# A hybrid attention, RWKV and gated-delta block on one core: wider tail products, and a fixed TensorE order of dense runs and small pieces

## Chip, cores, metric

The kernel runs on one core of a Trainium2 chip. The metric is the device time of one execution in microseconds (us); the median of three runs counts.

## What is computed

One transformer block over 1024 tokens of width 1024 in float32. The normalised input is projected once; three branches then mix the tokens, each of width 512, and a gated sum, an output projection and a feed-forward part follow:

```python
h = _rms(x, norm_mix_g[i])
proj = h @ w_in[i]
...
o_a = _nsa(...)      # 8 heads: compressed, selected and windowed attention
o_b, v_first = _rwkv7(...)   # 8 heads: a recurrence over the tokens
o_c = _gdn(...)      # 4 heads: a recurrence over chunks of the tokens
gate = jax.nn.sigmoid(p_gate.reshape(B, S, 3, D))
merged = (gate[:, :, 0] * (o_a @ w_branch[i, 0]) + gate[:, :, 1] * (o_b @ w_branch[i, 1])
          + gate[:, :, 2] * (o_c @ w_branch[i, 2]))
x = x + merged @ w_out[i]
h = _rms(x, norm_ffn_g[i])
x = x + jnp.square(jax.nn.relu(h @ w_ff1[i])) @ w_ff2[i]
```

## The kernel before

Large products are made from two halves of each operand: `whi` and `wlo` of a weight tile, `hTh` and `hTl` of the normalised input (`h2h`, `h2l` after the second norm, `fh`, `fl` of the hidden layer, `mh` and `ms` of the merged branches). Three matmuls of 128 x 128 weights per block make one product, and all add up in one PSUM tile `fps`. These are the **dense** matmuls. `load_w` fetches a weight tile (`wraw`), ScalarE casts it to `whi` (line 253), and GpSimd or VectorE or both subtract to get `wlo` (line 258); `TBUF` sets how many such pairs the tail keeps, `TRAW` how many raw tiles.

The **small pieces** are the matmuls and transposes of the three branches (`mps` tiles). They run in stages: RWKV up to 650 us (a step of its recurrence is `VS,AG`, then `xs,U`, then `VS,G`, with VectorE copies between), GDN from 690 to 1087 us (a step is `gZ,KQ`, `gxh,gU`, `gyb,gKg`; ahead of each unit a ladder of `gT`, `gU`, `gXb` inverts a triangular matrix), a preparation of the attention keys, then NSA with 32 units of two heads each (scores `K2s`, `K2w`, `K2c`; a VectorE maximum `ast`; a ScalarE exponential `P`; transposes of `P`; products `PH`, `PL` with the values).

A planner in the program, `Block.run`, emits the two kinds in turn. `Tensor` counts an estimated TensorE time; a task that yields a number is due again after that much estimated time. Small pieces add to `owed`, and where more than 0.64 us are owed, or no task is due, `dense_step` emits one step, which is three dense matmuls. Dense steps come from the branches' own projections and from a stock of 34 projections of gates and attention inputs (`waiting`), of which some are kept back (`keep`) until NSA begins. Emission is not yet the order: a scheduler behind it may move instructions by priority, and dense steps have a lower one. `Tensor.note` ties the first matmul of a dense step behind the last small piece emitted before it; nothing ties a small piece behind a dense one.

When the first half of NSA's units is emitted, `end_mixed` queues `tail(0)`: branch products, gates, output projection, second norm and feed-forward for the first 512 tokens, as dense work beside the second half of NSA. `tail(1)` does the same for the other 512 tokens at the end, where nothing else is left. Inside, `accum` adds products into the SBUF tile `acc`, 256 output columns at a time: for each of four row blocks all k steps run into one PSUM tile, then VectorE adds it to `acc`. The feed-forward part makes four hidden tiles (`up`, 24 matmuls each) and then their down products, eight groups per tail.

Of the kernel before, what the change touches and what calls it, by code (L numbers as in the profile page):

```python
# [42 lines left out]
FDIV = (0, 1)  # L43
TRAW = (2, 2)
TBUF = (2, 2)
# [3 lines left out]
OBUF = 5  # L49
# [32 lines left out]
class Tensor:  # L82
    EDGE = mybir.DependencyInfo(mybir.DependencyClass.NoSync, mybir.DependencyReason.DATA)

    def __init__(self, tc):
        self.tc, self.nc, self.time = tc, tc.nc, 0.0
        self.last = self.anchor = None
        self.dense = False

    def matmul(self, out, lhsT, rhs, **kw):  # L90
        m, n = lhsT.free_size(), out.free_size()
        if lhsT.dtype == F32:
            self.time += (2 * n + 64 if m <= 64 else 4 * max(n, P)) / 2400
        else:
            self.time += max(n, 64) / 2400
# [6 lines left out]
    def note(self, ins):  # L102
        if not self.dense:
            self.fresh = ins.ins
        elif self.anchor is not None:
            self.tc.add_manual_dep(ins.ins, self.anchor.name, self.EDGE, reason="dense step behind a small one")
            self.anchor = None
# [3 lines left out]
class Block:  # L111
# [54 lines left out]
    def run(self, until):  # L166
        now = lambda: self.te.time
        while not until():
            if self.owed > 0.64 and self.dense_step():
                self.owed -= 0.64  # L170
                continue
            can = [t for t in self.tasks if t.when is None or t.when()]
            due = [t for t in can if t.ready <= now()]
            if due:
# [5 lines left out]
                self.owed = min(self.owed + self.share * (now() - at), 2.0)  # L180
                if t.done:
                    self.tasks.remove(t)
            elif self.dense_step():
                self.owed = max(self.owed - 0.64, 0.0)
# [1226 lines left out]
    def tail(self, hf, wbufs):  # L1411
# [9 lines left out]
        def load(src, cols):  # L1421
            return self.load_w(src, 4, cols, wp, wbufs, TRAW[hf], div())

        with pool("tacc") as ap, pool("tw") as wp:
# [5 lines left out]
            def accum(lhs, w_rows, kt, c0):  # L1430
                ws = [load(w_rows[j * 512:(j + 1) * 512, c0:c0 + 256], 256) for j in range(kt // 4)]
                for st in range(4):
                    m = slice(st * P, (st + 1) * P)
                    ps = psum()[:, 0:256]
                    for k in range(kt):
                        (wh, wl), j = ws[k // 4], k % 4
                        self.te.matmul(ps, lhsT=lhs[0](k)[:, m], rhs=wh[:, j, :], start=(k == 0), stop=False)
                        self.te.matmul(ps, lhsT=lhs[0](k)[:, m], rhs=wl[:, j, :], start=False, stop=False)
                        self.te.matmul(ps, lhsT=lhs[1](k)[:, m], rhs=wh[:, j, :], start=False, stop=(k == kt - 1))
                        if k % 2:  # L1440
                            yield
                    tt(out=acc[:, st, c0:c0 + 256], in0=ps, in1=acc[:, st, c0:c0 + 256], op=OP.add)  # L1442
# [171 lines left out]
```

## Time and profile before

| | us |
|---|---|
| median of 3 runs | 2568.1 |
| lowest, highest | 2564.01, 2571.09 |
| profiled execution | 2570.32 |
| its span, first to last instruction | 2568.6 |
| TensorE matmuls busy | 2414.0 |
| VectorE busy | 1488.7 |
| ScalarE busy | 1044.3 |
| GpSimd busy | 989.9 |

Matmuls overlap in the records, so the time that one costs is the distance from its start to the next start, and not its duration. Idle time of TensorE is a stretch less its busy time. PE stands for TensorE, DVE for VectorE, ACT for ScalarE, POOL for GpSimd. A small float32 matmul appears as two records in the trace and as one row in the built order.

### The profile page before, as it was taken

How to read it: one execution, taken by the hardware profiler on the slowest of the kernel's cores; microseconds unless marked ns; L12 is line 12 of the kernel's file. 1: busy time of each engine (PE TensorE's matmuls, PEld its weight loads, DVE VectorE, ACT ScalarE, POOL GpSimd, SP SyncE). 2: the span in 40 equal slices, each digit the busy share in tenths (PEclk: the TensorE clock that was granted, in tenths of full speed). 3: DMA queues.
4: the chain of work that ended last, by engine and by line, in shares of the span. 5: the costliest groups of instructions: out<-in, count | busy, mean ns of one | idle time of the engine just before them, and what ended most of it. 6: DMA issues, size and time to landing. Idle time of an engine off the chain costs nothing.

```text
span 2568.6 us, 41137 instructions
## 1 busy us (share of the span) xinstructions
PE 2414.0 (94%) x15509; PEld 2013.4 (78%) x15509; DVE 1488.7 (58%) x3325; ACT 1044.3 (41%) x2085; POOL 989.9 (39%) x975
## 2 busy tenths in 40 slices
PE   7989899999898999989999999899999999999999
PEld 4767676777777777777887778788888878899988
DVE  4587877673576666223557787764454444545444
ACT  5333423332343333225667675753322333423232
POOL 4444433333322121234446675343332345223332
PEclk9889889999999999999999999899999999999999
DMA  4222222222223122362214331025322354223233
GB/s 135 66 54 66 57 52 66 70 55 79 67 66 83 40 54 76 114 137 76 61 50 141 101 102 37 20 72 154 95 91 86 104 160 132 78 87 107 83 104 102
DMA packets 340214, 217.05 MB, mean 84 GB/s; under 512 B 78486, under 2 KB 314144, under 8 KB 340016
## 3 DMA queue, kind: packets, MB, share of 16 engines
q1 hardware_dynamic: 329152, 195.63, 27.2%
q10 hardware_dynamic: 9792, 17.83, 1.9%
q8 instruction: 122, 2.00, 0.3%
q0 software_dynamic: 1072, 0.96, 0.2%
q14 instruction: 76, 0.62, 0.1%
HBM read 178.16 MB, written 36.22 MB: 83 GB/s over the span
## 4 chain that ended last, share of the span: by engine, by line
PE 71%; DVE 15%; DMA 6%; ACT 4%; issue 2%; POOL 1%; SPq 0%; ACTq 0%; DVEq 0%; POOLq 0%
PE fps L96 53%; PE mps L96 15%; PE mps L100 3%; DVE inv_p L335 2%; DVE inv_u L337 1%; DMA gin<-gates 1%; DVE BK L549 1%; DVE gacc L881 1%; DMA cw<-in_nsa_cmp_w_dram 1%; DMA lb<-inv 1%; ACT P L1348 1%; DMA inv<-LT 1%; DVE ast L1343 1%; DVE PL L1391 1%; DVE AG L536 1%
## 5 line engine op out<-in xcount | busy, mean ns | idle before, releaser
L258 POOL TENSOR_TENSOR wlo<-wraw,whi 128x512 fp32r<-128x512 f32 (+2 forms) x408 | 528.6, 1297 | 940.1 <-ACT whi L253 907.4
L253 ACT CAST whi<-wraw 128x512 fp32r<-128x512 f32 (+1 forms) x408 | 286.2, 703 | 699.5 <-PE fps L96 612.0
L96 PE MATMUL fps<-hTh,whi 128*128 128x512 f32 x1024 | 448.7, 440 | 6.7 <-ACT rraw L423 3.5
L96 PE MATMUL fps<-hTh,wlo 128*128 128x512 f32 x1024 | 416.4, 411 | 3.4 <-POOL wlo L258 3.4
L96 PE MATMUL fps<-hTl,whi 128*128 128x512 f32 x1024 | 418.1, 410 | 0.0
L96 PE MATMUL fps<-wlo,fh 128*128 128x256 f32 x1024 | 266.6, 284 | 7.0 <-DVE wlo L258 7.0
L96 PE MATMUL fps<-whi,fl 128*128 128x256 f32 x1024 | 266.7, 283 | 0.0
L96 PE MATMUL fps<-whi,fh 128*128 128x256 f32 x1024 | 266.0, 284 | 0.6
L258 DVE TENSOR_TENSOR wlo<-wraw,whi 128x256 fp32r<-128x256 f32 (+1 forms) x207 | 142.2, 690 | 180.2 <-ACT whi L253 180.1
L96 PEld LDWEIGHTS fps<-hTh,wlo 128*128 128x128 f32 x1024 | 200.7, 196 | 50.8 <-POOL wlo L258 5.2
L96 PEld LDWEIGHTS fps<-hTh,whi 128*128 128x128 f32 x1024 | 201.4, 197 | 49.0 <-ACT whi L253 3.8
L96 PEld LDWEIGHTS fps<-hTl,whi 128*128 128x128 f32 x1024 | 202.4, 198 | 32.5
L1442 DVE TENSOR_TENSOR acc<-fps,acc 128x256 f32<-128x256 f32 x288 | 118.6, 422 | 178.5 <-PE fps L96 178.1
L96 PE MATMUL fps<-h2h,whi 128*128 128x512 f32 x512 | 200.1, 391 | 0.9 <-DVE h2l L290 0.9
L96 PE MATMUL fps<-h2h,wlo 128*128 128x512 f32 x512 | 200.0, 391 | 0.2 <-DVE wlo L258 0.2
L96 PE MATMUL fps<-h2l,whi 128*128 128x512 f32 x512 | 199.8, 390 | 0.0
L1362 POOL TENSOR_SCALAR P<-P,ast 128x64 f32<-128x64 f32 (+5 forms) x128 | 138.6, 1100 | 144.7 <-DVE ast L1355 112.6
L96 PEld LDWEIGHTS fps<-wlo,fh 128*128 128x128 f32 x1024 | 186.3, 192 | 8.8 <-DVE wlo L258 8.4
L96 PEld LDWEIGHTS fps<-whi,fh 128*128 128x128 f32 x1024 | 186.9, 192 | 3.8 <-ACT whi L253 2.2
L96 PEld LDWEIGHTS fps<-whi,fl 128*128 128x128 f32 x1024 | 187.4, 192 | 0.1
L1348 ACT ACTIVATE P<-mps,ast 128x128 f32<-128x128 f32 (+4 forms) x256 | 125.1, 494 | 80.5 <-DVE ast L1346 47.3
L1343 DVE TENSOR_REDUCE ast<-mps 128x1 f32<-128x128 f32 (+4 forms) x256 | 109.0, 441 | 49.5 <-PE mps L96 47.3
(465 smaller groups left out, 4946.4 us busy)
## 6 DMA issues: line engine op xcount, KB each, us to landing
wraw<-in_w_in_dram SPq DMA_DIRECT2D x152, 256.0 KB, 2.9
wraw<-in_w_ff_dram SPq DMA_DIRECT2D x128, 256.0 KB, 2.9
wraw<-in_w_ff_dram SPq DMA_DIRECT2D x64, 512.0 KB, 3.4
gates<-fst ACTq DMA_DIRECT2D x48, 256.0 KB, 2.0
wraw<-in_w_branch_dram SPq DMA_DIRECT2D x48, 256.0 KB, 3.0
gin<-gates SPq DMA_DIRECT2D x48, 256.0 KB, 3.0
wraw<-in_w_out_dram SPq DMA_DIRECT2D x16, 512.0 KB, 3.6
nsa_in<-fst ACTq DMA_DIRECT2D x20, 256.0 KB, 2.1
```

The lines of the kernel that those rows point to most:

```text
L96: return self.note(self.nc.tensor.matmul(out, lhsT=lhsT, rhs=rhs, **kw))
L100: return self.note(self.nc.tensor.transpose(out, x, ident))
L253: nc.scalar.copy(hi, raw)
L258: eng.tensor_tensor(out=lo[:, x], in0=raw[:, x], in1=hi[:, x].bitcast(F32), op=OP.subtract)
L335: nc.vector.tensor_tensor(out=v, in0=lt[:n, s, None, s + 1:].to_broadcast([n, w, w]), in1=u[:n, s + 1:, s + 1:].rearrange("p t c -> p c t" ...
L337: nc.vector.tensor_reduce(out=u[:n, s, s + 1:], in_=v, axis=AX, op=OP.add)
L536: stt(out=ag[o, :, :, h], in0=ch2(sg)[o, :, c2], scalar=-1.0, in1=ch2(kk)[o, :, c2], op0=OP.mult, op1=OP.mult)
L549: tt(out=BK[HH[h], :, :, 1 - (x ^ h)], in0=ch2(t)[HH[h]], in1=ch2(WI)[HH[h]], op=OP.mult)
L1343: nc.vector.tensor_reduce(out=(mx if i == 0 else mx2)[:, b:b + 1], in_=ps[:, :n], axis=AX, op=OP.max, negate=True)
L1348: nc.scalar.activation(out=Pt[:, c:c + n], in_=tiles[i][:, :n], func=AF.Exp, bias=mx[:, b:b + 1], accum_out=(sm if i == 0 else sm2)[:, b:b ...
L1362: eng.tensor_scalar(out=Pt[:, c:c + n], in0=Pt[:, c:c + n], scalar1=r[:, b:b + 1], scalar2=None, op0=OP.mult)
L1442: tt(out=acc[:, st, c0:c0 + 256], in0=ps, in1=acc[:, st, c0:c0 + 256], op=OP.add)
```

## The change

Four things change. `accum` makes 512 output columns at a time from two weight tiles of two k blocks each, and the output projection adds each half of its k blocks to `acc` separately. Tile counts follow: the tails keep three and four pairs of weight tiles instead of two and two, `oh` and `ol` have four buffers instead of five, `fh` and `fl` five in the first tail instead of six, and raw branch tiles share three buffers with the gates. The planner emits dense steps three at a time (`RUN`), owes up to 4 us, and its estimate of a matmul grows by 32 columns and of each change of kind by 0.1 us. And `note` also ties every small piece behind the last dense matmul emitted before it, so that neither kind can pass the other.

```diff
+RUN = 3
+EDGE_US = 0.1
 TRAW = (2, 2)
-TBUF = (2, 2)
+TBUF = (3, 4)
 FSPLIT = (1, 1)
 FRAW = 2
 FBUF = 2
-OBUF = 5
+OBUF = 4
+FBUFS = (5, 6)
 ...
-            self.time += max(n, 64) / 2400
+            self.time += (max(n, 64) + 32) / 2400
 ...
+        if self.was != self.dense:
+            self.was = self.dense
+            self.time += EDGE_US
         if not self.dense:
             self.fresh = ins.ins
-        elif self.anchor is not None:
-            self.tc.add_manual_dep(ins.ins, self.anchor.name, self.EDGE, reason="dense step behind a small one")
-            self.anchor = None
+            if self.run is not None:
+                self.tc.add_manual_dep(ins.ins, self.run.name, self.EDGE, reason="small piece behind a dense run")
+        else:
+            self.run = ins.ins
+            if self.anchor is not None:
+                self.tc.add_manual_dep(ins.ins, self.anchor.name, self.EDGE, reason="dense step behind a small one")
+                self.anchor = None
         return ins
 ...
-            if self.owed > 0.64 and self.dense_step():
-                self.owed -= 0.64
-                continue
+            if self.owed > RUN * 0.68:
+                at = now()
+                if any([self.dense_step() for _ in range(RUN)]):
+                    self.owed -= now() - at
+                    continue
 ...
-                self.owed = min(self.owed + self.share * (now() - at), 2.0)
+                self.owed = min(self.owed + self.share * (now() - at), 4.0)
 ...
-            elif self.dense_step():
-                self.owed = max(self.owed - 0.64, 0.0)
+            elif any([self.dense_step() for _ in range(RUN)]):
+                self.owed = max(self.owed - RUN * 0.68, 0.0)
 ...
-            def accum(lhs, w_rows, kt, c0):
-                ws = [load(w_rows[j * 512:(j + 1) * 512, c0:c0 + 256], 256) for j in range(kt // 4)]
+            def accum(lhs, w_rows, k0, c0):
+                ws = [load(w_rows[(k0 + j) * P:(k0 + j + 2) * P, c0:c0 + 512], 2, 512) for j in (0, 2)]
                 for st in range(4):
                     m = slice(st * P, (st + 1) * P)
-                    ps = psum()[:, 0:256]
-                    for k in range(kt):
-                        (wh, wl), j = ws[k // 4], k % 4
-                        self.te.matmul(ps, lhsT=lhs[0](k)[:, m], rhs=wh[:, j, :], start=(k == 0), stop=False)
-                        self.te.matmul(ps, lhsT=lhs[0](k)[:, m], rhs=wl[:, j, :], start=False, stop=False)
-                        self.te.matmul(ps, lhsT=lhs[1](k)[:, m], rhs=wh[:, j, :], start=False, stop=(k == kt - 1))
-                        if k % 2:
-                            yield
-                    tt(out=acc[:, st, c0:c0 + 256], in0=ps, in1=acc[:, st, c0:c0 + 256], op=OP.add)
+                    ps = psum()
+                    for k in range(4):
+                        (wh, wl), j = ws[k // 2], k % 2
+                        self.te.matmul(ps, lhsT=lhs[0](k0 + k)[:, m], rhs=wh[:, j, :], start=(k == 0), stop=False)
+                        self.te.matmul(ps, lhsT=lhs[0](k0 + k)[:, m], rhs=wl[:, j, :], start=False, stop=False)
+                        self.te.matmul(ps, lhsT=lhs[1](k0 + k)[:, m], rhs=wh[:, j, :], start=False, stop=(k == 3))
+                        yield
+                    tt(out=acc[:, st, c0:c0 + 512], in0=ps, in1=acc[:, st, c0:c0 + 512], op=OP.add)
 ...
-                            raw = op.tile([P, 512], F32, name="or", tag="or", bufs=2)
+                            raw = op.tile([P, 512], F32, name="or", tag="gin", bufs=3)
 ...
-                            g = op.tile([P, 512], F32, name="gin", tag="gin", bufs=2)
+                            wh, wl = load(a["w_branch"][0, b][:, dt * P:(dt + 1) * P], 4, P)
+                            g = op.tile([P, 512], F32, name="gin", tag="gin", bufs=3)
 ...
-                for c0 in range(0, D, 256):
-                    yield from accum(lhs, a["w_out"][0], KT, c0)
+                for c0 in range(0, D, 512):
+                    for k0 in range(0, KT, 4):
+                        yield from accum(lhs, a["w_out"][0], k0, c0)
 ...
-                        hi = fp.tile([P, 512], F32R, name="fh", tag="fh", bufs=6)
-                        lo = fp.tile([P, 512], F32R, name="fl", tag="fl", bufs=6)
+                        hi = fp.tile([P, 512], F32R, name="fh", tag="fh", bufs=FBUFS[hf])
+                        lo = fp.tile([P, 512], F32R, name="fl", tag="fl", bufs=FBUFS[hf])
 ...
-                        for c0 in range(0, D, 256):
-                            yield from accum(lhs, a["w_ff2"][0][g * P:(g + G) * P, :], G, c0)
+                        for c0 in range(0, D, 512):
+                            yield from accum(lhs, a["w_ff2"][0][g * P:(g + G) * P, :], 0, c0)
```

In the built order TensorE changes from a small piece to dense matmuls 601 times before and 488 times after. Runs of exactly nine dense matmuls number 35 before and 263 after, runs of one to six 431 and 170.

TensorE in the middle of RWKV before, between two products of the recurrence (`xs,U`, then `VS,G`, then `VS,AG`):

```order
L96 MATMUL mps<-xs,U_3880 64x64 x4
L96 MATMUL mps<-VS,G 64x64
L96 MATMUL mps<-VS,KB 64x64 x4
L96 MATMUL mps<-VS,G 64x64 x3
L96 MATMUL fps<-hTh,whi 128x512
L96 MATMUL fps<-hTl,whi 128x512
L96 MATMUL fps<-hTh,wlo 128x512
L96 MATMUL mps<-VS,AG 64x64 x8
```

and near the end of RWKV after:

```order
L100 MATMUL mps<-xs,U_5869 64x64 x4
L100 MATMUL fps<-hTh,whi 128x512
L100 MATMUL fps<-hTl,whi 128x512
L100 MATMUL fps<-hTh,wlo 128x512
L100 MATMUL fps<-hTh,whi 128x512
L100 MATMUL fps<-hTl,whi 128x512
L100 MATMUL fps<-hTh,wlo 128x512
L100 MATMUL mps<-VS,G 64x64
L100 MATMUL mps<-VS,KB 64x64 x4
L100 MATMUL mps<-VS,G 64x64 x3
```

Where `VS,G` stood right behind `xs,U`, six dense matmuls now stand between them.

TensorE in the last steps of GDN's recurrence before:

```order
L96 MATMUL mps<-gyb,gKg 128x128
L96 MATMUL mps<-gyb,gQK 128x128
L96 MATMUL fps<-hTh,whi 128x512
L96 MATMUL fps<-hTl,whi 128x512
L96 MATMUL fps<-hTh,wlo 128x512
L96 MATMUL mps<-gZ,KQ 128x128
L96 MATMUL fps<-hTh,whi 128x512
L96 MATMUL fps<-hTl,whi 128x512
L96 MATMUL fps<-hTh,wlo 128x512
L96 MATMUL fps<-hTh,whi 128x512
L96 MATMUL fps<-hTl,whi 128x512
L96 MATMUL fps<-hTh,wlo 128x512
```

and the last rows of GDN after:

```order
L100 MATMUL mps<-gZ,KQ 128x128 x2
L100 MATMUL mps<-gxh,gU 128x128
L100 MATMUL mps<-gyb,gKg 128x128
L100 MATMUL mps<-gyb,gQK 128x128
L100 MATMUL mps<-gZ,KQ 128x128 x2
L100 MATMUL mps<-gxh,gU 128x128
L100 MATMUL mps<-gyb,gKg 128x128
L100 MATMUL mps<-gyb,gQK 128x128
L104 MATMUL mps<-ident,gO 128x128 x4
L100 MATMUL fps<-hTh,whi 128x512
```

The dense matmuls between the hops are gone from the last steps; they stand earlier.

TensorE in the first half of NSA before:

```order
L100 MATMUL mps<-ident,P 128x128 x4
L96 MATMUL fps<-hTh,whi 128x512
L96 MATMUL fps<-hTl,whi 128x512
L96 MATMUL fps<-hTh,wlo 128x512
L96 MATMUL mps<-PH,V2c 128x256
L96 MATMUL fps<-hTh,whi 128x512
L96 MATMUL mps<-PL,V2c 128x256
L100 MATMUL mps<-ident,P 128x128 x4
L96 MATMUL mps<-K2s,QH 128x512
L96 MATMUL mps<-K2s,QL 128x512
L96 LDWEIGHTS identb
L96 MATMUL mps<-mtri,identb 128x128
```

and in the same half after:

```order
L100 MATMUL mps<-K2w,QH 128x256
L100 MATMUL mps<-K2w,QL 128x256
L100 LDWEIGHTS identb
L100 MATMUL mps<-mtri,identb 128x128
L100 MATMUL mps<-K2c,QH 128x64
L100 MATMUL mps<-K2c,QL 128x64
L100 LDWEIGHTS identb
L100 MATMUL mps<-mcmp,identb 128x64
L100 MATMUL mps<-K2s,QH 128x384
L100 MATMUL mps<-K2s,QL 128x384
L100 LDWEIGHTS identb
```

The first half of NSA held 384 dense matmuls before; after, 30 stand at its start and 713 small ones follow without a dense one among them.

## Rows read from the trace of the kernel before

**Rows 1.** The page: busy time of TensorE; shares of the chain by engine.

```profile
PE 2414.0 (94%) x15509; PEld 2013.4 (78%) x15509; DVE 1488.7 (58%) x3325; ACT 1044.3 (41%) x2085; POOL 989.9 (39%) x975
...
PE 71%; DVE 15%; DMA 6%; ACT 4%; issue 2%; POOL 1%; SPq 0%; ACTq 0%; DVEq 0%; POOLq 0%
```

**Rows 2.** Busy time by stretch: RWKV, GDN, NSA's two halves, the second tail.

```profile
core 0: us, PE busy (x) PEld busy (x) DVE busy (x) ACT busy (x) POOL busy (x), PEclk, DMA share, GB/s
61.00:650.00 589.00, 547.94 (x4156) 411.48 (x4155) 398.93 (x950) 199.21 (x381) 237.62 (x239) 0.91 0.25 62
...
690.00:1087.00 397.00, 360.11 (x2171) 295.18 (x2169) 245.03 (x672) 147.52 (x248) 87.14 (x102) 0.96 0.26 68
...
1181.50:1383.00 201.50, 196.27 (x1161) 160.52 (x1159) 115.72 (x315) 131.31 (x359) 105.90 (x109) 0.98 0.24 75
1383.00:1735.00 352.00, 332.25 (x2159) 283.44 (x2158) 262.88 (x592) 229.26 (x568) 201.01 (x145) 0.98 0.23 72
...
2205.00:2564.00 359.00, 359.00 (x2304) 328.25 (x2303) 172.53 (x291) 107.77 (x162) 113.83 (x94) 1.00 0.31 94
```

**Rows 3.** TensorE's waits in RWKV, GDN, NSA's second half: us, times, longest.

```profile
PE mps L96 <- DVE VS L698: 6.7, 5, 1.7
PE mps L96 <- DVE BK L549: 6.2, 3, 4.0
...
PE mps L96 <- DVE gZ L1068: 3.9, 3, 1.6
...
PE mps L100 <- DVE gT L1014: 1.2, 1, 1.2
...
PE mps L96 <- ACT P L1348: 7.5, 9, 1.7
```

**Rows 4.** Timeline of TensorE in RWKV: start, length, what, [idle before <-releaser].

```profile
194.64 0.38 PE L96 MATMUL mps<-VS,G 128*64 128x64 f32 x2 [1.66 <-DVE VS L698]
...
570.30 0.90 PE L96 MATMUL mps<-VS,AG 64*64 64x64 f32 x5 [1.48 <-DVE VS L704]
```

**Rows 5.** Timeline of TensorE in the second tail.

```profile
2295.84 0.28 PE L96 MATMUL fps<-wlo,fh 128*128 128x256 f32 x1
...
2300.28 0.28 PE L96 MATMUL fps<-whi,fl 128*128 128x256 f32 x1
...
2302.01 0.39 PE L96 MATMUL fps<-h2l,whi 128*128 128x512 f32 x1
...
2309.04 0.39 PE L96 MATMUL fps<-h2h,wlo 128*128 128x512 f32 x1
```

**Rows 6.** Groups by line, whole span: count | busy us, mean ns | idle.

```profile
L96 PE MATMUL fps<-whi,fh 128*128 128x256 f32 x1024 | 266.0, 284 | 0.6
...
L96 PE MATMUL fps<-whi,mh 128*128 128x256 f32 x256 | 71.0, 288 | 0.0
```

**Rows 7.** The first tail, 1735 to 2066: a group, and a timeline row.

```profile
L96 PE MATMUL fps<-wlo,fh 128*128 128x256 f32 x474 | 113.1, 284 | 7.0 <-DVE wlo L258 7.0
...
1786.22 0.62 PE L96 MATMUL fps<-wlo,fh 128*128 128x256 f32 x3 [1.16 <-DVE wlo L258]
```

**Rows 8.** Timeline of TensorE near the end of GDN.

```profile
1062.65 0.38 PE L96 MATMUL mps<-gZ,KQ 128*128 128x128 f32 x2
...
1063.01 0.47 PE L96 MATMUL fps<-hTh,whi 128*128 128x512 f32 x1
1063.32 0.39 PE L96 MATMUL fps<-hTl,whi 128*128 128x512 f32 x1
...
1067.24 0.38 PE L96 MATMUL mps<-gZ,KQ 128*128 128x128 f32 x2
```

**Rows 9.** Stretches almost without dense work; one of three dense groups, 1181.5:1383.

```profile
1356.60:1383.00 26.40, 23.09 (x137) 18.14 (x135) 21.49 (x54) 19.56 (x57) 18.15 (x16) 0.87 0.62 205
1641.00:1672.00 31.00, 25.05 (x136) 19.66 (x136) 22.66 (x61) 27.57 (x63) 5.29 (x6) 0.78 0.04 12
...
L96 PE MATMUL fps<-hTh,whi 128*128 128x512 f32 x128 | 54.1, 424 | 0.2 <-ACT fst L321 0.2
```

More of the change, by code (lines that the diff above doesn't have):

```diff
@@ L86, in __init__ @@
         self.tc, self.nc, self.time = tc, tc.nc, 0.0
-        self.last = self.anchor = None
-        self.dense = False
+        self.last = self.anchor = self.run = None
+        self.dense = self.was = False
     def matmul(self, out, lhsT, rhs, **kw):
@@ L1419, in tail, with load @@
         div = lambda: TDIV[hf] if self.tasks else TDIV[1]
-        def load(src, cols):
-            return self.load_w(src, 4, cols, wp, wbufs, TRAW[hf], div())
+        def load(src, kt, cols):
+            return self.load_w(src, kt, cols, wp, wbufs, TRAW[hf], div())
         with pool("tacc") as ap, pool("tw") as wp:
@@ L1458, in tail @@
                         for dt in range(KT):
-                            wh, wl = load(a["w_branch"][0, b][:, dt * P:(dt + 1) * P], P)
-                            g = op.tile([P, 512], F32, name="gin", tag="gin", bufs=2)
+                            wh, wl = load(a["w_branch"][0, b][:, dt * P:(dt + 1) * P], 4, P)
+                            g = op.tile([P, 512], F32, name="gin", tag="gin", bufs=3)
                             nc.sync.dma_start(out=g, in_=self.gates[b * KT + dt, :, T])
@@ L1492, in up @@
                         for kh in range(2):
-                            wh, wl = load(a["w_ff1"][0][kh * 512:kh * 512 + 512, ft * P:(ft + 1) * P], P)
+                            wh, wl = load(a["w_ff1"][0][kh * 512:kh * 512 + 512, ft * P:(ft + 1) * P], 4, P)
                             for j in range(4):
```

## Prediction

> **What bounds the kernel now.** I read the page's busy times and chain first: TensorE is busy for 94% of the span and its matmuls are 71% of the chain that ended last [rows 1]. So time can go in two ways only: fewer TensorE microseconds for the same products, or less TensorE idle time. Then the stretches by stage [rows 2]: in the last one, from 2205 us, TensorE is never idle (359.00 of 359.00 us), and the stretch is nothing but tail products. Where small pieces and dense products share TensorE, it idles 41 us in the RWKV stage (589.0 less 547.9), 37 us in GDN, 5 us in the first half of NSA and 20 us in the second. TensorE's granted clock there is 0.91 of full speed in RWKV and 0.96 in GDN, a mean of its two levels 1.2 and 2.4 GHz, so about 18% of the RWKV stage, 106 us, runs at 1.2 GHz. Who TensorE waits for: VectorE results of the recurrences in RWKV and GDN, and the exponentials of NSA [rows 3]. Last, the timeline around such waits [rows 4]. I went through all waits of a small piece over 0.1 us in RWKV, GDN and the second half of NSA: 82 with 89 us. In 42 of them (42 us) the piece stood right behind another small piece, in 28 (29 us) behind a dense run of six matmuls or fewer, in 12 (18 us) behind a longer run. Of the two rows shown one is of the first kind and one of the second.
>
> **1. 512 columns instead of 256.** In the stretch without idle time 37 starts of 256-column matmuls lie between 2295.84 and 2300.28, that is 0.120 us each; 31 starts of 512-column ones lie between 2302.01 and 2309.04, 0.2268 us each [rows 5]. Two of the former cost 0.240, one of the latter 0.227: 13 ns less. There are 3 x 1024 + 3 x 256 = 3840 matmuls of 256 columns [rows 6], which become 1920. 1920 x 0.0132 = 25 us, nearly all of it where TensorE has no idle time, so it counts in full: **-25**. The accumulating adds on VectorE go from 288 of half width to 160 of full width; VectorE is busy for half of that stretch [rows 2], and I cost them at nothing. The Trainium skill has a formula for this spacing (page TensorE: Matmul & The Clock Gate, section Back-to-back issue gap): N/2.4 ns plus a fixed 2.5 ns, so 109 ns for 256 columns and 216 for 512. By it the change would save 2.6 ns a pair, an estimate of 5 us in all. The trace has 120 and 227, so it differs, and I go by the rows; the page's result is a rival below.
>
> **2. Weight buffers of the tail.** In the first tail's feed-forward part every group of four loses 1.2 us at its first down product, waiting for VectorE's half of `wlo`: 7.0 us in that stretch [rows 7]. Three buffers instead of two let that split run a tile earlier: -7 if all of it goes. Against it, each accumulation now holds two of the three buffers, and its successor's second tile can be split only when the last row block has left the first one, about 2.7 us (12 matmuls of 0.227) before it is needed. If that is 0.6 us too late in each of 20 accumulations it costs +12. I take **-4**. The branch products lose one `oh` buffer (five to four) at two boundaries per half: 0 to +6, taken as 0, since the next raw tile is still fetched ahead.
>
> **3. Fewer changes between small and dense.** The built order has 601 entries from a small piece into a dense run before and 488 after. The first dense matmul behind a small one takes 0.31 us to the next start (1063.01 to 1063.32) instead of 0.227 [rows 8]: 0.08 us, with the change back about 0.1. Most of the difference lies in NSA's first half and is in the next term; elsewhere it is 510 against 483, so **-3**.
>
> **4. NSA's first half loses its dense work.** Longer runs use up the stock of gate projections sooner. In the built order 354 dense matmuls that stood in this half now stand earlier; 30 are left at its start, and behind them come 713 small matmuls in a row. Their 80 us of TensorE time are only moved. What counts is how long the small pieces take alone. Now the stage lasts 201.5 us with 1161 matmuls, of which 385 are dense [rows 2, 9]; 385 x 0.227 = 87, so 114 us go to 776 small ones and the changes between them. The trace shows the same work without dense cover: between 1356.6 and 1383 TensorE runs 137 small pieces in 26.4 us, 5.19 per us at clock 0.87 [rows 9]. 776 / 5.19 = 150 us: **+35**. Bounds: if only VectorE's 116 us set the pace, +2; by the other thin stretch (1641 to 1672, 136 matmuls in 31 us, 4.39 per us, clock 0.78) it is 177 us, +63. I take the first stretch since it is the same half and piece size.
>
> **5. The end of GDN loses its dense work too.** A step of this recurrence now lasts 4.6 us (1062.65 to 1067.24) and holds 15 dense matmuls, 3.4 us [rows 8]. After, the last four steps and one ladder of the inverse stand without dense work. If a step keeps its length for latency alone, 4 x 3.4 = 14 us are idle, and five hops of the ladder of about 1 us (a wait for `gT` is 1.2 us, for `gZ` 1.3 on average) [rows 3] add 5; if it falls to its own matmuls, nothing. I take **+10**, nearer the upper end, since each of the three hops crosses VectorE.
>
> **6. Waits of small pieces.** Dense runs of nine become 263 (35 before), runs of one to six fall from 431 to 170. Nine matmuls are 2.04 us; the single waits are mostly 1 to 2 us [rows 3]. A piece that stood behind six or fewer gets 0.7 to 1.8 us more cover: I let half of these 29 us go. Of the 42 us behind another small piece I let a third go: there the order put the piece ahead of dense matmuls that had been emitted before it, and that is now forbidden. Together **-28**. Bounds: -57 if the first kind goes altogether and the second by two thirds; +15 if merged small groups (fewer changes mean longer ones) wait more than now. The price of the rule is delay: a small piece can stand 2 us behind a run that is itself waiting for a weight split, and VectorE and ScalarE behind it. In RWKV, where VectorE is busy for 399 of 589 us, there is room.
>
> **7. The clock.** Less idle time in RWKV should hold 2.4 GHz longer; of 106 us at 1.2 GHz I count a tenth of the time lost as regained: **-10**, between 0 and -40.
>
> Sum: -25 - 4 - 3 + 35 + 10 - 28 - 10 = -25. The profiled execution took 2570.3 us (span 2568.6, 1.7 around it), 2 us over the median 2568.1. 2570 - 25 = **2545 us**, 0.9% under the median. About 0.3% (8 us) is what a measurement of this kernel can tell from no change.
>
> **Rivals.**
> (a) Slower: NSA's first half alone crawls. One place, 713 pieces with nothing between them, each waiting for reduction, exponential, cast. By the 4.39 row the term is +63 instead of +35, and if half of these pieces, 57 of their 114 us, ran at 1.2 GHz where they now run at 2.4, up to 57 us more; I take 30. 2545 + 28 + 30 = **2603 us**. It decides from a rate under 4.5 pieces per us, which lies between the two thin rows. For it: clock 0.87 and 0.78 there. Against: the row of the same half gives 5.19. Chance 0.19. The Trainium skill (same page, Loop structure matters more than you think) warns of matmuls with a wait between each two, which it expects to run cold; the trace agrees in part, with 0.87 and 0.78 rather than 0.5.
> (b) No gain: the waits come back behind merged small groups, so term 6 is about 0 and term 7 too: 2545 + 28 + 10 = 2583, and with the weight-buffer stall gone and the end of GDN free, **2570 us**. Chance 0.14.
> (c) Faster: the rule does for the recurrences what it says. Term 6 at -50, the clock regains 25, NSA alone needs 140 us: 2545 - 22 - 15 - 10 = **2498 us**. For it: 2.04 us exceed nearly every wait listed. Chance 0.22.
> (d) The width saves nothing much, 5 instead of 25 us, as a fixed small cost per matmul would have it: **2565 us**. Against: 68 starts in a row [rows 5]. Chance 0.03.
> That the order is not what the change says can be ruled out: it stands in the built program.
>
> **How the numbers follow.** Forecast 2545 (2528 to 2562 by small errors of the terms), chance 0.42. Under 2560: nearly all of it and (c), 0.62. Within 8 us of 2568: (b) mostly, (d) and an edge of the forecast, 0.17. Above 2576: (a) and a little of (b), 0.21. The range runs from 2495, (c), to 2600, most of (a).
>
> **What would show it.** Right: starts of 512-column products 0.227 us apart to the end, the pure tail some 25 us shorter for its work; a stretch of about 150 us with no dense matmul in NSA; TensorE idle in RWKV under 30 us. Wrong: that stretch over 175 us, or RWKV idle at 41 us or more, or waits for `wlo` and `whi` at every accumulation of the first tail.

## The result, and the profile after

The changed kernel takes 2707.57 us (median of 4 runs, 2706.85 to 2718.84) and the kernel before 2566.06 us (4 runs, 2561.18 to 2571.09). The ratio is 1.056, with a 95% interval of 1.053 to 1.060: 141 us slower, where 2545 us and a gain were forecast. The range ended at 2600 us.

The first row of the page after, whose counterpart is in [rows 1]:

```profile
PE 2446.4 (90%) x13589; PEld 1954.0 (72%) x13589; DVE 1472.9 (54%) x3180; ACT 1042.5 (39%) x2077; POOL 996.8 (37%) x975
```

The profiled span is 2706.4 us. Span less TensorE's busy time is its idle time: 260.0 us, against 2568.6 - 2414.0 = 154.6 before. So of the 137.8 us by which the span grew, 105.4 are idle time. Busy time grew by 32.4, though the dense work became cheaper. Next the windows of the changed kernel by stage (the columns of [rows 2]): RWKV, GDN, the two halves of NSA, the middle of the first tail, the second tail.

```profile
core 0: us, PE busy (x) PEld busy (x) DVE busy (x) ACT busy (x) POOL busy (x), PEclk, DMA share, GB/s
68.00:750.10 682.10, 584.15 (x4284) 443.52 (x4284) 401.51 (x948) 192.19 (x378) 242.76 (x245) 0.88 0.24 59
788.00:1199.00 411.00, 369.75 (x2176) 302.34 (x2175) 249.08 (x672) 151.50 (x250) 89.09 (x102) 0.94 0.24 64
1346.20:1500.20 154.00, 133.05 (x793) 106.42 (x791) 108.69 (x310) 109.19 (x316) 83.06 (x93) 0.88 0.14 46
1500.20:1973.40 473.20, 429.13 (x2270) 344.26 (x2270) 295.74 (x622) 257.61 (x609) 234.39 (x167) 0.94 0.22 67
1973.40:2216.00 242.60, 239.70 (x1052) 197.93 (x1052) 111.77 (x155) 74.36 (x111) 81.43 (x68) 0.99 0.34 108
2353.00:2701.50 348.50, 348.50 (x1539) 288.21 (x1536) 163.60 (x225) 107.30 (x160) 114.45 (x92) 1.00 0.30 97
```

RWKV is idle for 97.95 us, where [rows 2] had 41, and its granted clock fell from 0.91 to 0.88. The second half of NSA is idle for 44.07 us (20 before), its clock 0.94 (0.98). The second tail still has no idle time at all.

Stages can't be compared by their lengths, because the change moves dense work between them. So I counted the dense matmuls in each stage in both traces, priced them at the distances between starts of [rows 5] (0.227 us for 512 columns, 0.120 for 256) and took that off the length. What is left, the "rest", holds the small pieces, the idle time and what a lower clock costs. The time at 1.2 GHz is worked out from the granted clock, a mean of 1.2 and 2.4 GHz: stage length times twice what the clock lacks to 1. The stretches between the stages are left out.

| us | length before, after | dense before, after | rest before, after | difference of rest | at 1.2 GHz before, after |
|---|---|---|---|---|---|
| RWKV | 588.6, 682.2 | 274.7, 304.0 | 313.9, 378.2 | +64 | 104, 167 |
| GDN | 387.1, 408.1 | 227.7, 230.4 | 159.4, 177.7 | +18 | 27, 46 |
| preparation | 103.8, 150.1 | 57.7, 101.9 | 46.2, 48.2 | +2 | 14, 16 |
| NSA, first half | 201.6, 154.0 | 87.2, 6.8 | 114.4, 147.2 | +33 | 7, 38 |
| NSA, second half | 352.1, 473.2 | 152.5, 224.2 | 199.6, 249.0 | +49 | 14, 55 |
| rest of the tails | 833.4, 733.1 | 794.7, 698.1 | 38.7, 34.9 | -4 | 8, 17 |

At these prices all dense work of the program fell from 1643.7 to 1617.6 us, 26 less. RWKV and the second half of NSA, the two stages for which a gain was forecast, lost 113 us together.

Who TensorE waits for in RWKV after, and then in the second half of NSA (us in total, times, longest):

```profile
PE mps L100 <- DMA T<-inv: 35.9, 8, 15.3
PE mps L100 <- ACT U L652: 14.5, 7, 3.4
PE mps L100 <- DVE VS L711: 7.6, 5, 2.5
PE mps L100 <- ACT sg L518: 6.7, 8, 1.6
PE mps L104 <- DVE T L643: 6.4, 2, 4.0
```

```profile
PE mps L100 <- ACT P L1361: 11.5, 7, 4.3
PE fps L100 <- POOL ol L271: 9.8, 5, 3.0
PE mps L100 <- DVE PL L1404: 7.0, 12, 1.6
```

The first line is new. `T<-inv` brings the inverses of the 16-wide diagonal blocks of a RWKV unit's triangular matrix: VectorE works them out (around line 350) in its own small layout, and transfers through DRAM bring them to `T`, where the products `T,L` (32 records for a unit) want them. Before, that wait was 1.2 us in the whole stage; now it is 35.9:

```profile
PE mps L96 <- DMA T<-inv: 1.2, 2, 0.8
```

The waits of [rows 3] for `VS` and `P` didn't go either: 6.7 became 7.6, and 7.5 became 11.5.

The timeline shows what became of it. First TensorE before, around the first unit's `T,L` (start, length, what, [idle before <-releaser]), then TensorE after, at the same place in the program:

```profile
151.98 0.71 PE L96 MATMUL mps<-AG,BK 64*128 64x128 f32 x4
...
164.81 1.13 PE L96 MATMUL mps<-AG,BK 64*128 64x128 f32 x8 [0.33 <-DVE G L586]
167.14 0.79 PE L100 MATMUL mps<-ident,BK 128*128 128x128 f32 x4 [1.21 <-DVE G L586]
168.28 0.44 PE L96 MATMUL mps<-T,L 64*64 64x64 f32 x2 [0.35 <-DMA T<-inv]
168.65 1.11 PE L100 MATMUL mps<-ident,BK 128*128 128x128 f32 x4
169.56 1.06 PE L100 MATMUL mps<-ident,rkv 128*128 128x128 f32 x4
170.55 1.97 PE L96 MATMUL mps<-T,L 64*64 64x64 f32 x30
```

```profile
161.36 0.50 PE L100 MATMUL fps<-hTh,wlo 128*128 128x512 f32 x1 [0.47 <-POOL wlo L271]
...
162.18 0.40 PE L100 MATMUL fps<-hTh,wlo 128*128 128x512 f32 x1
177.91 0.44 PE L100 MATMUL mps<-T,L 64*64 64x64 f32 x2 [15.33 <-DMA T<-inv]
```

Before, other work stands ahead of `T,L` until its input is there, and the group is even split: two of its matmul records, eight transposes, then the other 30. Much of that work are the next unit's own small pieces: its `AG,BK` products start at 152.0, 16 us ahead of this `T,L`. After, they start 20 us behind it, at 197.8; the dense run ends at 162.2 us, and TensorE stands still for 15.3 us with `T,L` at its head.

What the prediction said of the spacing in the tail did come. Starts of 512-column products in the second tail, 18 steps over 4.08 us, are 0.227 us apart. These ones had 512 columns before too; for those that changed the whole second tail tells. From its first `h2h,whi` to its last matmul it took 359.0 us with 2304 matmuls before, and takes 348.1 with 1536 now, 0.227 for each: 10.9 us less for 768 pairs made into one. And the first tail's wait for `wlo` of 7.0 us [rows 7] has become one of 2.9 for `whi`:

```profile
2499.81 0.39 PE L100 MATMUL fps<-h2l,whi 128*128 128x512 f32 x1
...
2503.89 0.39 PE L100 MATMUL fps<-h2l,whi 128*128 128x512 f32 x1
```

```profile
L100 PE MATMUL fps<-whi,fh 128*128 128x512 f32 x192 | 67.0, 395 | 2.9 <-ACT whi L266 2.9
```

### The profile page after: what moved, and what is told of

Read it like the earlier page. It is cut to its first block, busy times and chain, and to the rows that moved or that the text cites. A ratio compares the mean times of both kernels' runs of the same rounds, so it can differ in the third digit from the quotient of the medians.

```text
span 2706.4 us, 37150 instructions
## 1 busy us (share of the span) xinstructions
PE 2446.4 (90%) x13589; PEld 1954.0 (72%) x13589; DVE 1472.9 (54%) x3180; ACT 1042.5 (39%) x2077; POOL 996.8 (37%) x975
## 5 line engine op out<-in xcount | busy, mean ns | idle before, releaser
L271 POOL TENSOR_TENSOR wlo<-wraw,whi 128x512 fp32r<-128x512 f32 (+2 forms) x408 | 534.3, 1311 | 1095.3 <-ACT whi L266 1066.3
L100 PE MATMUL fps<-hTh,whi 128*128 128x512 f32 x1024 | 454.2, 448 | 10.1 <-ACT rraw L436 3.5
L271 DVE TENSOR_TENSOR wlo<-wraw,whi 128x256 fp32r<-128x256 f32 (+1 forms) x190 | 117.1, 619 | 208.8 <-ACT whi L266 201.9
L100 PE MATMUL fps<-whi,fh 128*128 128x512 f32 x512 | 192.6, 395 | 2.9 <-ACT whi L266 2.9
L100 PE MATMUL fps<-whi,fl 128*128 128x512 f32 x512 | 192.0, 390 | 0.0
L100 PE MATMUL fps<-wlo,fh 128*128 128x512 f32 x512 | 190.6, 390 | 0.0
L1454 DVE TENSOR_TENSOR acc<-fps,acc 128x512 f32<-128x512 f32 x160 | 107.4, 686 | 115.0 <-PE fps L100 114.7
L1404 DVE TENSOR_TENSOR PL<-mps,PH 128x512 fp32r<-128x512 f32 (+2 forms) x168 | 103.1, 618 | 31.8 <-ACT PH L1403 30.7
L348 DVE TENSOR_TENSOR inv_p<-lb,inv_u 64x1 f32<-64x1 f32 (+29 forms) x240 | 96.7, 403 | 41.8 <-DMA lb<-inv 35.9
L1403 ACT CAST PH<-mps 128x512 fp32r<-128x512 f32 (+2 forms) x168 | 88.4, 531 | 73.2 <-PE mps L104 70.0
```

The lines of the kernel that those rows point to most:

```text
L100: return self.note(self.nc.tensor.matmul(out, lhsT=lhsT, rhs=rhs, **kw))
L271: eng.tensor_tensor(out=lo[:, x], in0=raw[:, x], in1=hi[:, x].bitcast(F32), op=OP.subtract)
L348: nc.vector.tensor_tensor(out=v, in0=lt[:n, s, None, s + 1:].to_broadcast([n, w, w]), in1=u[:n, s + 1:, s + 1:].rearrange("p t c -> p c t" ...
L1403: nc.scalar.copy(PH[:n, x0:x1], ps[:n, x0:x1])
L1404: tt(out=PL[:n, x0:x1], in0=ps[:n, x0:x1], in1=PH[:n, x0:x1].bitcast(F32), op=OP.subtract)
L1454: tt(out=acc[:, st, c0:c0 + 512], in0=ps, in1=acc[:, st, c0:c0 + 512], op=OP.add)
```

## The experiments

These theories stood against each other. **The tie** (T): the new rule, a small piece behind the last dense matmul emitted before it, costs the time. Its rivals are the other parts: the runs of three (R), the planner's new estimate (E), and the wider products with their buffers. If it is the tie, then there are two ways. **Order** (O): the planner's emitted order becomes the order of execution, and its waiting times are too short, so that pieces come to TensorE's head before their inputs. **Delay** (D): a piece that is ready is held back by the dense run ahead of it. All kernels compute everything.

### Which part of the change

**The changed kernel without the tie.**

```diff
-            if self.run is not None:
-                self.tc.add_manual_dep(ins.ins, self.run.name, self.EDGE, reason="small piece behind a dense run")
```

> The changed kernel without the tie that puts every small piece behind the last dense matmul; runs of three steps, the new estimate and the 512-column tail stay. Theory T (the tie costs the time: a small piece that is ready stands behind 2 us of dense work, its VectorE and DMA followers start later, and the next piece finds its input missing): most of the 140 us come back, 2570 to 2600 us, and TensorE's wait for the inverse through DRAM (T<-inv, 36 us in RWKV) falls under 10 us. Theory R (the runs of three steps cost it, whoever orders them): 2670 to 2710 us, the wait stays over 25 us.

Measured: 2565.68 us over 8 runs, 1.000 of before (0.998 to 1.002). The span is 2563.9 us and TensorE's busy time 2409.8, so it idles 154.1 us, as before. The two lines that were taken out are worth 142 us, a little more than T expected. RWKV, and the wait for the inverse in it:

```profile
61.00:691.40 630.40, 585.27 (x4314) 446.14 (x4314) 393.26 (x951) 207.71 (x396) 242.75 (x247) 0.90 0.26 64
```

```profile
PE mps L100 <- DMA T<-inv: 3.2, 3, 2.7
```

With nearly the same dense work in the stage as the changed kernel has (311 against 304 us) it is idle for 45 us instead of 98, and the wait for `T<-inv` is 3.2 us.

**The kernel before with the tie and nothing else.** The same lines, put into `note` of the kernel before.

> The kernel before with the tie alone: single dense steps, 256 columns, the old estimate. T: slow, 2640 to 2700 us, with RWKV waits of small pieces of 80 us or more. R: 2560 to 2600 us, since without long runs a tied piece is held up 0.7 us at most.

Measured: 2737.95 us, 1.067 (1.063 to 1.071), 171 us slower with the very instructions of before (15509 matmul records in both). The page, RWKV, and its waits:

```profile
PE 2448.7 (89%) x15509; PEld 2026.0 (74%) x15509; DVE 1475.8 (54%) x3325; ACT 1036.2 (38%) x2075; POOL 986.1 (36%) x975
```

```profile
67.20:742.60 675.40, 551.24 (x4131) 414.19 (x4131) 394.45 (x948) 183.56 (x365) 237.00 (x238) 0.87 0.22 54
```

```profile
PE mps L96 <- DMA T<-inv: 77.0, 15, 14.5
PE mps L96 <- ACT U L643: 18.4, 8, 3.2
```

The idle time is 2738.2 - 2448.7 = 289.5 us, 135 more than before; the busy time rose by 34.7 at a mean granted clock of 0.945 (0.964 before). The tie alone does what the whole change does, and more than T expected. By stage the rest grew by 92 us in RWKV, 55 in the second half of NSA, 10 in GDN, 8 in the first half of NSA.

The planner doesn't see the tie, so in this kernel and in the one before it emitted the same order. Here that order is kept, and the first unit's `T,L` comes ahead of the next unit's `AG,BK`:

```profile
170.48 0.44 PE L96 MATMUL mps<-T,L 64*64 64x64 f32 x2 [8.94 <-DMA T<-inv]
...
186.22 0.48 PE L96 MATMUL mps<-AG,BK 64*128 64x128 f32 x2
```

Before, the scheduler had put these `AG,BK` first, at 151.98 and `T,L` at 168.28, and it did so at three of the seven changes of unit. With the tie it happens at none.

**The changed kernel with the planner's old estimate.**

```diff
-            self.time += (max(n, 64) + 32) / 2400
+            self.time += max(n, 64) / 2400
-EDGE_US = 0.1
+EDGE_US = 0.0
```

> The changed kernel with the old estimate of TensorE time (no 32 columns and no 0.1 us for a change of kind). Theory E (the planner's waiting times are counted on its own clock; a clock that charges more per matmul lets fewer real microseconds pass for the same waiting time, so pieces are emitted before their inputs are there): 2630 us or less, T<-inv under 20 us. T and R: within 20 us of 2707.

Measured: 2724.83 us, 1.062 (1.058 to 1.066). E wanted 2630 us or less. With the tie in place the new estimate isn't the cause; it gives the changed kernel 17 us. RWKV's rest is 369.0 us here and 378.2 with the new estimate, while the first half of NSA is worse off, 161.5 against 147.2.

**The wider products and their buffers alone.** `accum`, the tile counts and the weight buffers as in the change; `note`, the estimate and `Block.run` as before:

```diff
 ...
+            if self.owed > 0.64 and self.dense_step():
+                self.owed -= 0.64
+                continue
-            if self.owed > RUN * 0.68:
-                at = now()
-                if any([self.dense_step() for _ in range(RUN)]):
-                    self.owed -= now() - at
-                    continue
 ...
```

> The planner and the order of before, with the 512-column tail and its buffers. My sum of terms 1 and 2 gives -29: 2538 us, interval 2530 to 2548, with 512-column starts 0.227 us apart and the 1.2 us stall per group of the first tail gone. If the width itself were at fault (adds of double width, two weight tiles held per accumulation): 2566 us or more.

Measured: 2533.3 us over 4 runs (2532.08 to 2546.39), 0.989 (0.985 to 0.993): 33 us faster than before, beside -29 by terms 1 and 2 of the prediction. It is the fastest kernel of this study and beats both the kernel before and the changed one. RWKV is nearly as it was:

```profile
61.60:647.20 585.60, 540.80 (x4156) 407.50 (x4156) 398.12 (x951) 198.68 (x379) 232.81 (x238) 0.92 0.26 62
```

### What the tie does: order or delay

Against delay speaks a count. From a small piece's last input (by its semaphore) to its start, where a dense run stood in between, RWKV's pieces lost 1.10 us on average before, 0.90 with the tie alone and 1.12 in the changed kernel (in each of the two later ones two products `gd,upg`, whose inputs had been there for over 60 us, are left out). Only in the second half of NSA is there a part of it: 0.58, 0.75 and 0.99. For order speaks the inverse. From the end of a unit's last `AG,BK` to its first `T,L` it takes 34 to 48 us before and 32 to 45 after: the chain is as long as ever, and what differs is whether TensorE has other work in that time. The planner's entry for it, `LAT[5]`, is 16 us. That is no time on the chip, since the planner counts its own estimate of TensorE's time: with the tie alone, `T,L` stood at TensorE's head 28 to 38 us after the last `AG,BK`, and waited for the rest.

**The tie alone, with 36 us for the inverse.**

```diff
-LAT = (0.0, 10.0, 0.2, 0.3, 0.1, 16.0, 1.2, 1.2, 1.2, 1.2, 1.0, 9.0, 4.0)
+LAT = (0.0, 10.0, 0.2, 0.3, 0.1, 36.0, 1.2, 1.2, 1.2, 1.2, 1.0, 9.0, 4.0)
```

> The kernel before with the tie (as e2) and one planner number changed: the waiting time for RWKV's inverse is 36 us instead of 16. In every run the products with the inverse start 30 to 48 us after the last AG,BK product, so 16 is far too short. Theory O (the tie freezes the planner's own order, and that order puts pieces where their inputs are not there yet): T<-inv falls from 77 us to under 15, the kernel gains 40 us or more against e2, to 2700 us or less. Theory D (a tied small piece is held back by the dense run ahead of it, so all that follows it, the inverse too, comes later): T<-inv stays over 40 us and the time within 20 us of 2738.

Measured: 2749.8 us, 1.070 (1.066 to 1.074). Against 1.067 (1.063 to 1.071) with 16 us that is no gain, where order promised 40 us; the time came as delay had it. The wait for `T<-inv`, 77.0 us, is gone from the list of waits, as order says, but others took its place, and RWKV became longer:

```profile
PE mps L100 <- POOL Y L738: 18.2, 4, 7.4
PE fps L96 <- POOL wlo L262: 15.2, 11, 3.2
PE mps L96 <- ACT U L643: 14.2, 7, 3.9
```

```profile
65.70:770.50 704.80, 604.07 (x4290) 461.78 (x4290) 398.62 (x948) 192.54 (x380) 242.74 (x246) 0.85 0.23 58
```

It holds 36 us more dense work, and its rest fell by 7 us only: TensorE idles 101 us there instead of 124, but at a clock of 0.85 instead of 0.87. A unit of RWKV takes about 63 us before (from one first `AG,BK` to the next), 77 with the tie, 82 here. In the first six of the eight units `T,L` now starts 59 to 67 us after the last `AG,BK`, though the transfers had landed 40 to 48 us after it, 13 to 25 us earlier. So there the entry is no longer too short but too long. To name the largest wait isn't to name the cost, and neither theory has all of it.

**The tie alone, with the short waits doubled too.** The entries of one product to the next, in the tables of all three branches:

```diff
-LAT = (0.0, 10.0, 0.2, 0.3, 0.1, 16.0, 1.2, 1.2, 1.2, 1.2, 1.0, 9.0, 4.0)
+LAT = (0.0, 10.0, 0.2, 0.3, 0.1, 36.0, 2.4, 2.4, 2.4, 2.4, 2.0, 9.0, 4.0)
-GLAT = (8.0, 3.0, 2.5, 0.5, 0.3, 20.0, 1.2, 0.8, 0.5, 6.0)
+GLAT = (8.0, 3.0, 2.5, 0.5, 0.3, 20.0, 2.4, 1.6, 1.0, 6.0)
-NLAT = (1.5, 3.0, 6.0, 0.3, 1.0, 3.0, 6.0, 0.6, 2.0, 0.8)
+NLAT = (1.5, 3.0, 6.0, 0.3, 1.0, 3.0, 6.0, 1.2, 2.0, 1.6)
```

> As e5, and the planner's waiting times for the short hops of RWKV, GDN and NSA doubled (1.2 to 2.4 us, 0.8 to 1.6, 0.6 to 1.2 and the like). O: waits for single VectorE and ScalarE results shrink too, another 20 to 50 us under e5, idle time of TensorE in RWKV under 60 us (124 in e2). D: no better than e5, or slower, since more dense matmuls per hop lengthen the chains.

Measured: 2678.66 us, 1.042 (1.039 to 1.046): 59 us less than the tie alone, 71 less than with the inverse's entry alone, which is more than order expected. TensorE idles 65 us in RWKV (60 expected, 124 with the tie alone). RWKV and the largest waits in it:

```profile
67.00:714.70 647.70, 583.03 (x4290) 451.73 (x4290) 409.82 (x949) 192.25 (x380) 242.54 (x245) 0.87 0.25 63
```

```profile
PE mps L96 <- ACT U L643: 16.9, 7, 5.1
PE mps L100 <- POOL Y L738: 10.1, 3, 8.6
```

RWKV's rest is 342.2 us (406.2 with the tie alone, 313.9 before), that of the second half of NSA 227.9 (255.0 and 199.6). The planner's times do decide, under the tie: with the same rule and the same work, longer ones give a third of the loss back (59 of 171). Delay had expected nothing under 2750 us.

**The changed kernel with these times.**

> The changed kernel itself with the planner's longer waiting times of e6 (36 us for the inverse, short hops doubled). O, as far as e6 bore it out (2738 to 2679 there): 2635 to 2670 us, T<-inv under 5 us instead of 36, non-dense time of RWKV 340 us or less instead of 378 and of NSA's second half 230 or less instead of 249. D: no better than 2700.

Measured: 2664.2 us, 1.038 (1.035 to 1.041), 43 us less than the changed kernel. Again a third of what the tie costs there (43 of 142). Its idle time is 2659.1 - 2433.9 = 225.2 us, against 260.0. The time is as expected, the places are so in part: the wait for `T<-inv` is down to 6.5 us (5 expected), but RWKV's rest is still 366 us (340 expected) and that of the second half of NSA 235 (230 expected), while GDN's, which nobody had named, fell from 178 to 164.

**The wider products without the tie, with these times.** The control: are longer times good in themselves?

> e4 (columns alone, no tie) with the same longer waiting times. O says that a scheduler free to move small pieces past dense work repairs the planner's short numbers, so that longer ones gain little here: 2520 to 2560 us against 2533. A gain of over 20 us would say that short numbers cost time without the tie as well; a loss of over 40 us that more dense work per hop is harmful in itself.

Measured: 2586.55 us, 1.007 (1.004 to 1.009), 53 us slower than the wider products with the old times. Without the tie the same numbers harm, so their gain above belongs to the tie. The profiled execution is the longest of the six (2598.69 us; granted clocks 0.943 to 0.953). In it the idle time is nearly the same, 158.6 us against 151.0; TensorE's busy time rose by 57, the mean granted clock fell from 0.965 to 0.943, and RWKV shows it:

```profile
61.30:723.90 662.60, 611.78 (x4314) 457.06 (x4314) 396.37 (x950) 210.07 (x397) 243.60 (x246) 0.88 0.24 61
```

RWKV holds 36 us more dense work there, but 71 us more busy time than with the old times. The expectation reads such a loss as harm by more dense work for each hop. The amount in the stage isn't it: the changed kernel without the tie has the same 311 us of it in RWKV, and the stage takes 630.4 us there against 662.6. What it is in its place wasn't looked into.

**The tie alone, with the short waits four times as long.** If the tie's cost were only a matter of too short times, still longer ones should go on giving back.

In place of the first values:

```diff
+LAT = (0.0, 10.0, 0.2, 0.3, 0.1, 36.0, 4.8, 4.8, 4.8, 4.8, 4.0, 9.0, 4.0)
+GLAT = (8.0, 3.0, 2.5, 0.5, 0.3, 20.0, 4.8, 3.2, 2.0, 6.0)
+NLAT = (1.5, 3.0, 6.0, 0.3, 1.0, 3.0, 6.0, 2.4, 2.0, 3.2)
```

> The kernel before with the tie, 36 us for the inverse and the short hops at four times their first value. If the planner's numbers were all there is to the tie's cost, the order should now be safe: TensorE's idle time in RWKV under 45 us (before: 41, e6: 65), 2640 us or less. If part of the cost is the frozen order itself (a chain can only go on in the row that was written down for it): 2670 us or more, though waits for single results shrink.

Measured: 2715.74 us, 1.058 (1.055 to 1.061), 37 us slower than with twice. The second half of NSA has one wait of a small piece left (0.7 us), but its rest is still 232.3 us and its idle time 40.5, nearly all of it before dense work. GDN's rest is 203 us (173 with twice), and RWKV has not become free of waits:

```profile
PE mps L96 <- ACT U L643: 15.8, 6, 5.5
PE mps L96 <- DVE VS L702: 12.5, 14, 2.5
```

```profile
65.80:731.40 665.60, 586.39 (x4290) 459.79 (x4290) 398.86 (x948) 198.13 (x384) 239.52 (x246) 0.85 0.24 61
```

So of the lengths tried twice is the best, and the tie still costs about 110 us there (1.042 of before). Too short times are at least a third of the loss by these runs. What the rest is stays open. Times that are now too long are part of it in some places, as GDN suggests. That a piece whose input comes early cannot go up, and one whose input comes late holds everything behind it, whatever one number a table has for it, would fit too, but no run here separates the two.

### What the other two parts cost without the tie

**Runs of three, with the wider products and the old estimate, without the tie.** The kernel without the tie, and the old estimate in it:

```diff
-            self.time += (max(n, 64) + 32) / 2400
+            self.time += max(n, 64) / 2400
-EDGE_US = 0.1
+EDGE_US = 0.0
```

> The changed kernel without the tie and with the old estimate: so the 512-column tail and runs of three steps. Against e4 (2533, single steps) and e1 (2566, runs of three and the new estimate). If the runs cost the 33 us between these two, through the dense stock that is gone in NSA's first half: 2555 to 2575 us, non-dense time of that half 130 us as in e1 (115 in e4). If the estimate costs them: 2530 to 2545.

Measured: 2585.04 us over 8 runs, 1.007 (1.005 to 1.010).

**The new estimate with the wider products alone.**

```diff
-            self.time += max(n, 64) / 2400
+            self.time += (max(n, 64) + 32) / 2400
-EDGE_US = 0.0
+EDGE_US = 0.1
```

> e4 (columns alone) with the new estimate of TensorE time added, single steps, no tie. The other side of e7: if runs of three are the cause there, 2525 to 2545 us here; if the estimate is, 2555 or more. By the built order more dense work is left for NSA's first half (529 matmuls instead of 385), so idle time should not rise there.

Measured: 2582.15 us over 10 runs, 1.005 (1.003 to 1.006).

Each by itself costs 40 to 50 us on top of the wider products (by the ratios to the kernel before 1.007 for the runs, 1.005 for the estimate, against 0.989), both together 32 us (2566). Both expectations fell: neither part can be named as the one that costs it. The estimate alone spends less dense work in RWKV (263 us against 275) and leaves more for NSA (120 against 87 in the first half). The runs of three spend 311 us in RWKV and leave 44, and so does the kernel with both, so their joint effect is not a sum of the two. Why each costs that much isn't settled. About half is idle time, +21 us for the runs and +27 for the estimate, and half busy time at a lower clock (0.951 and 0.947 against 0.965). The places differ: the first half of NSA has a rest of 135 us with the runs of three (115 without), and TensorE's idle time in GDN is 51 us with the estimate (29 without).

## Why the prediction was wrong, point by point

1. **512 columns: right.** -25 forecast. The second tail, never idle, lost 10.9 us with 768 of the 1920 pairs, 14 ns each, and the part alone with its buffers brought 33 us. (The 26 us of dense work in the table above are the forecast's own prices times the counts, so they confirm nothing; and the sign of a second tail some 25 us shorter was put wrongly, since that stretch holds only these 768.) By the formula of the Trainium skill (page TensorE: Matmul & The Clock Gate, section Back-to-back issue gap), which that section gives for an isolated matmul, it would have been an estimate of 5 us, at 2.5 ns a pair; the trace disagrees with the formula at both widths, 0.120 and 0.227 us.
2. **Weight buffers: the stall went, the gain didn't show.** -4 forecast. Waits for `wlo` in the two tails fell from 8.0 to 1.3 us, and instead of a wait at every accumulation there is a single new one, of 2.9 us for `whi`. But the branch products wait 7.7 us there for `oh` and `ol` (0.3 before), which the term took as 0; the wider products alone show the same, 8.5 us. TensorE's idle time in the tails is 22.7 us before and 23.4 after. The -4 of the table is no more than its prices are good for.
3. **Fewer changes: not told apart.** -3 is too little to be seen in a rest that moved by 64.
4. **NSA's first half alone: right.** The rest grew by 33 us for a forecast of 35. 793 matmul records in 154.0 us are 5.15 per us, and the row it was costed from had 5.19. The rival (a) named the wrong place: this half didn't crawl, at a granted clock of 0.88. The Trainium skill (same page, Loop structure matters more than you think) expects matmuls with a long DMA wait before each to run cold. The waits here are short ones for other engines, 21 us in all, and it holds in part: at 0.88 about a quarter of the stretch, 38 of 154 us, ran at 1.2 GHz.
5. **The end of GDN: right in its idle time, low in size.** +10 forecast with bounds 0 and about 19; +18 measured over the whole stage. Idle time rose by 10 us, all of it in the last 40 us of the stage, where there was none before. What the term left out is the clock: 0.72 in these 40 us, 1.00 before. The tie has a part in it that the term didn't see: without it the stage's rest is 159.4 us, as before, though its end is nearly as bare (14 us of dense work in the last 40; 8 with the tie, 33 before).
6. **Waits of small pieces: this step failed.** It gave -28 between -57 and +15. RWKV and the second half of NSA lost 113 us in place of the 38 that terms 6 and 7 forecast as gain; their idle time, which this term priced, rose by 57 and 24 us. The forecast took each wait of before as a thing that more dense cover would shorten, and saw that the order put pieces ahead of dense matmuls that had been emitted earlier; it counted 42 us of waits behind such pieces as the harm of that passing. It was the reverse. Freedom to pass kept TensorE in work that was ready, as the next unit's `AG,BK` ahead of `T,L` shows, and the waits were what remained after it; forbidding it costs 142 us with the rest of the change and 171 alone. In the changed kernel, 42 of RWKV's 50 waits of a small piece, 52 us, and all 26 in the second half of NSA, 23 us, stand right behind another small piece, where no dense run covers them. Of RWKV's others five, 31 us, stand behind a dense run longer than six, which was not long enough; the 15.3 us for `T<-inv` are among them. The prediction's own sign of being wrong, RWKV idle at 41 us or more, came with 98. The upper bound failed for the same reason: it came from the waits that existed, and the wait that became the largest, for `T<-inv`, had 1.2 us in that list. The trace of before held a warning: from `AG,BK` to `T,L` a unit takes 34 to 48 us there, and the next unit's small pieces stand in between, ahead of a `T,L` that had been emitted before them.
7. **The clock: wrong in sign.** -10 was forecast. The time at 1.2 GHz went from 104 to 167 us in RWKV and from 14 to 55 in the second half of NSA. It rose where the idle time rose; term 7 rested on term 6 alone. This is part of the 113 us, not on top of them.

One reading was loose: of the 18 us of waits behind longer runs 5.8 are for an input transfer at the end of GDN, but they enter no term.

In sum: -26 for the dense work, +33 for NSA's first half, +18 for GDN, +2 and -4 for the preparation and the tails, and +113 where -38 was expected. That is 136 of the 138 us of the span. That the dense work and the first half of NSA came out as forecast is no luck, their prices were read from rows of the same work; the sum failed on terms 6 and 7. The rival (b), that the waits come back, was right in kind, but its price stopped at the waits of before, which gave 2570 us.

## What to carry to other kernels

Where a planner emits an order from a table of waiting times and a scheduler behind it may still let ready work pass, short entries of the table need not cost anything: without the tie, longer ones made the kernel slower here. A rule that freezes the emitted order turned too short entries into stalls of the engine, and doubling them gave back only a third. Before such a rule is priced, look in the trace for pieces that run ahead of others emitted before them, and price the waits that would come, not only those that are there. An entry counts on the planner's own clock, so compare it with when the piece reaches the engine. And take a wide change apart: the wider products with their buffers alone (2533 us) were the gain, and the three other parts hid it.

## What the runs showed of the hardware that was not expected

- The granted clock can fall with hardly more idle time. The wider products with longer planner times idle for 158.6 us and with the old times for 151.0, yet the mean granted clock is 0.943 and 0.965, and TensorE's busy time is 57 us longer for the same work. Most plainly in RWKV: with the longer times it idles 50.8 us at a clock of 0.88, and with the runs of three, without the tie and with the old estimate, 52.2 us at 0.92, both with 311 us of dense work. What sets them apart wasn't looked into further.
- The way of the 16-wide inverses through VectorE and DRAM back to TensorE is long: with the tie alone their transfers landed 29 to 49 us after the last product before them, and the first product behind them stood waiting.
- 256 columns cost 0.120 us from start to start and 512 cost 0.227, so narrow products of this kind lose 13 ns in each pair; over the 768 pairs of the second tail 10.9 us were measured.
